# Padding in front of the MLP's inner activations: their SBUF addresses get the weight tiles' remainder modulo 512 bytes

## The chip, the cores and the metric

One core of one Trainium2 chip runs the whole program in one launch. The metric is the device time of one execution in microseconds (us), as the median over several runs. Engines are named as in the profile: PE is TensorE (PEld its weight loads), DVE is VectorE, ACT is ScalarE, POOL is GpSimd, SP issues most DMAs. SBUF addresses below are byte offsets within a partition, and "remainder" always means such an address modulo 512.

## The reference, cut to what matters

A decoder trunk of two layers works on 256 positions of width 2048, in float32. Each layer is a token mixer, a cross-attention to a memory of 256 positions, and an MLP, each behind an RMS norm and added to its input:

```python
for i in range(DEPTH):                      # DEPTH = 2
    h = rms_norm(x, g_mix[i])
    x = x + (chunked_gmlp(h, ...) if i % 2 == 0 else s5_glu(h, ...))
    x = x + memory_attention(rms_norm(x, g_xattn[i]), rms_norm(mem, g_mem[i]), ...)
    x = x + squared_relu_mlp(rms_norm(x, g_ff[i]), f_w_up[i], f_w_down[i])

def squared_relu_mlp(h, w_up, w_down):      # w_up 2048 x 8192, w_down 8192 x 2048
    return jnp.square(jax.nn.relu(h @ w_up)) @ w_down
```

The change lies in the MLP of both layers.

## The kernel before, in words

**How a product is made.** Every float32 operand of a large product is split into a high part in the type fp32r and a low part that holds the rest. A product is then three fp32r products: high by high, high by low, low by high. Weights stream from HBM in blocks of 512 KB (128 partitions by 1024 numbers). `wload` puts a block into one of four `wraw` tiles; `split` (L101, L102) lets ACT write the high part `whi` and DVE the low part `wlo`, of which there are three buffers each. On PE a matmul has a stationary operand, 128 columns that are loaded as weights, and a moving operand that streams past it, here 512 or 256 columns. All matmuls below are issued one after the other with the next one's weight load in between.

**The three shapes of the loop over a block.**
- `gemm_tok` (L145 to L147) multiplies activations in the large `act` tile with a weight block: the activations are stationary (`ah`, `al`), the weights move. It serves the mixers and the attention.
- `gemm_feat` (L163, L165) has it the other way round: the weights are stationary, the activations of `act` move. L163 takes high and low activations in one matmul of 512 columns, L165 one of 256. It makes the MLP's hidden values, and the attention's q and k.
- `gemm_hid` (L558 to L560) is written like `gemm_tok`, with the MLP's hidden values as stationary operand. These lie in tiles `hh` (high) and `hl` (low), four of each, that `mlp` allocates in a pool of its own. `gemm_last` (L579 to L581) does the same work for the very last quarter of columns in layer 1, with split weights that lie in two tiles `last`.

The inner lines of `gemm_tok` and of `gemm_hid`, in this order, are

```python
nc.tensor.matmul(out[t], ah[:, kt, sl], hi[:, kk, :], start=st, stop=False)             # L145
nc.tensor.matmul(out[t], ah[:, kt, sl], lo[:, kk, :], start=False, stop=False)          # L146
nc.tensor.matmul(out[t], al[:, kt, sl], hi[:, kk, :], start=False, stop=en)             # L147

nc.tensor.matmul(acc[:, t, :], ah[:, kt % 4, sl], hi[:, kk, :], start=st, stop=False)   # L558
nc.tensor.matmul(acc[:, t, :], ah[:, kt % 4, sl], lo[:, kk, :], start=False, stop=False)# L559
nc.tensor.matmul(acc[:, t, :], al[:, kt % 4, sl], hi[:, kk, :], start=False, stop=en)   # L560
```

The second argument is the stationary operand, the third the moving one. One weight block feeds 12 such matmuls, four groups of three; a group of three is called a triple below.

**The MLP.** The hidden width of 8192 is done in four rounds `b`. A round makes 2048 hidden values with eight calls of `gemm_feat` (each ends in a small `r` tile, from which ACT and DVE make `hh` and `hl`), and then multiplies them with a quarter of `f_w_down` in four calls of `gemm_hid`, 128 triples. In layer 0 the setup of the state-space mixer runs beside the MLP as small pieces (`side` work: DVE arithmetic, small matmuls, DMAs from POOL). In the last round of layer 1, the last 32 triples are those of `gemm_last`.

**What sets addresses.** Tiles of a pool lie one behind the other in the order in which they are first allocated, each start rounded up to 32 bytes. In the pool of `mlp` the first tile is `r2`, 8 bytes per partition, then come four `hh`, four `hl` and two `r`. The sizes of these are multiples of 512 bytes, so that all of them have one remainder, which depends on where the pool starts and on the size of `r2`. Columns are sliced from `act`, `hh`, `hl`, `whi` and `wlo` at multiples of 512 bytes, so the remainder of every operand of L145 to L147, L163, L165 and L558 to L560 is that of its tile.

**What sets the order.** The order on each engine is that of the program text, with side work put in at fixed ticks (one tick per weight block).

Of the kernel before, what the change touches and what calls it, by code (L numbers as in the profile page):

```python
# [9 lines left out]
F32 = mybir.dt.float32  # L10
# [6 lines left out]
P = 128  # L17
# [21 lines left out]
class Trunk:  # L39
# [470 lines left out]
    def mlp(self, x, layer, cur, nxt):  # L510
        nc, a, tc = self.nc, self.a, self.tc
        wu, wd = a["f_w_up"][layer], a["f_w_down"][layer]
        hT = cur.act
        with tc.tile_pool(name="ml", bufs=4, reuse_waits="tile") as mp:
            r2 = mp.tile([P, 2], F32, name="r2", bufs=1)
            for b in range(DFF // D):
                hid = []
                for n in range(NCH):
                    h = mp.tile([P, 4, S], F32R, name="hh")
                    l = mp.tile([P, 4, S], F32R, name="hl")  # L520
                    for i in range(2):
                        r = mp.tile([P, 2, S], F32, name="r", bufs=2)
                        self.gemm_feat(hT, wu, 2 * (NCH * b + n) + i, r)
                        nc.vector.scalar_tensor_tensor(out=r, in0=r, scalar=0.0, in1=r, op0=ALU.max, op1=ALU.mult)  # L524
                        self.split(h[:, 2 * i:2 * i + 2], l[:, 2 * i:2 * i + 2], r)
                    hid.append((h, l))
                if b == 0:
                    rstd = cur.rstd()
                    nc.vector.tensor_tensor(out=r2, in0=rstd, in1=rstd, op=ALU.mult)
                if b == DFF // D - 1:  # L530
                    nxt.start()
                for n in range(NCH):
                    if nxt.closing and b == DFF // D - 1 and n == NCH - 1:
                        self.gemm_last(hid, wd, n, b * KT, lambda t, acc: (
                            nc.vector.scalar_tensor_tensor(  # L535
                                out=x[:, t, n * NB:], in0=acc, scalar=r2[:, t:t + 1],
                                in1=x[:, t, n * NB:], op0=ALU.mult, op1=ALU.add), nxt.finish(x, t)))
                        break
                    acc = self.gemm_hid(hid, wd, n, b * KT)
                    for t in range(2):  # L540
                        xc = x[:, t, n * NB:(n + 1) * NB]
                        nc.vector.scalar_tensor_tensor(out=xc, in0=acc[:, t, :], scalar=r2[:, t:t + 1], in1=xc,  # L542
                                                       op0=ALU.mult, op1=ALU.add)
                    if b == DFF // D - 1:
                        self.at(1, lambda n=n: nxt.chunk(x, n))
# [647 lines left out]
```

## Time and profile before

| | |
|---|---|
| median of 3 runs | 2884.1 us (2883.07 to 2889.95) |
| the profiled execution's own time | 2886.18 us |
| its span, first to last instruction | 2884.4 us |
| PE busy in the span | 2837.0 us (98%) |
| DVE, ACT busy | 1831.7 us (64%), 1332.5 us (46%) |
| DMA | 579.55 MB, mean 201 GB/s |

A span is one execution on the core. A matmul's recorded duration (about 395 ns) overlaps that of the next, so the pace of a stream is read from start to start and not from durations. The MLP of layer 0 runs from about 690 to 1444 us of the span, that of layer 1 from 2155 to 2871 us.

### The profile page before, as it was taken

To read this page: it belongs to the slowest core of one execution; us is meant where nothing else is said; L and a number is where in the kernel's file an instruction comes from. 1 tells how busy PE (TensorE), PEld (TensorE's weight loads), DVE (VectorE), ACT (ScalarE), POOL (GpSimd) and SP (SyncE) were. 2 spreads that over 40 slices of the span, in tenths; PEclk is the share of its full clock that TensorE was granted. 3 is DMA by queue.
4 is the path that set the end of the run, shared out by engine and by line. 5 is a ranking of instruction groups with operands and counts; after the bars stand their busy time and mean duration, and the time that the engine had idled before them with its cause. 6 is when DMAs were issued, how large, how long until landed. Compare 5 with 4: busy or idle time off the path is not lost.

```text
span 2884.4 us, 39580 instructions
## 1 busy us (share of the span) xinstructions
PE 2837.0 (98%) x15238; PEld 2365.6 (82%) x15238; DVE 1831.7 (64%) x2548; ACT 1332.5 (46%) x1714; POOL 205.4 (7%) x384
## 2 busy tenths in 40 slices
PE   8999999999999999999989999999999999999998
PEld 6778888888878888788867788888888888888886
DVE  5665655575778878787567566555556555465555
ACT  5445544444534444444455445444454344343443
POOL 1000000000022222222011000000000000000000
PEclk9999999999999999999999999999999999999999
DMA  8656655558677777777689766655566566666665
GB/s 276 216 187 192 195 176 175 176 175 232 193 215 212 224 218 222 214 219 207 214 243 281 224 201 210 184 175 183 173 185 190 188 186 188 187 192 185 188 188 148
DMA packets 180461, 579.55 MB, mean 201 GB/s; under 512 B 37440, under 2 KB 39664, under 8 KB 179504
## 3 DMA queue, kind: packets, MB, share of 16 engines
q1 hardware_dynamic: 140864, 509.67, 57.3%
q0 software_dynamic: 39264, 67.29, 8.6%
q8 instruction: 119, 1.95, 0.3%
q14 instruction: 70, 0.57, 0.1%
q10 hardware_dynamic: 144, 0.07, 0.0%
HBM read 553.88 MB, written 22.94 MB: 200 GB/s over the span
## 4 chain that ended last, share of the span: by engine, by line
PE 90%; DMA 4%; DVE 3%; issue 2%; ACT 1%; POOL 0%; SPq 0%; DVEq 0%; ACTq 0%; POOLq 0%
PE acc L163 24%; PE acc L165 12%; PE acc L560 8%; PE acc L559 8%; PE acc L558 8%; PE acc L146 8%; PE acc L147 8%; PE acc L145 8%; DVE wlo L102 1%; DMA wraw<-in_b_w_in 1%; PE ps L494 1%; PE ps L438 1%; PE ps L214 1%; DMA memc<-in_mem 1%; DMA wraw<-in_f_w_up 0%
## 5 line engine op out<-in xcount | busy, mean ns | idle before, releaser
L102 DVE TENSOR_TENSOR wlo<-wraw,whi 128x1024 fp32r<-128x1024 f32 x952 | 1164.4, 1224 | 859.6 <-ACT whi L101 857.2
L101 ACT CAST whi<-wraw 128x1024 fp32r<-128x1024 f32 x952 | 999.5, 1051 | 1314.1 <-PE acc L163 394.0
L163 PE MATMUL acc<-act,whi 128*128 128x512 f32 x3072 | 1080.4, 395 | 0.6 <-ACT whi L101 0.6
L165 PE MATMUL acc<-act,wlo 128*128 128x256 f32 x3072 | 866.1, 282 | 1.7 <-DVE wlo L102 1.6
L163 PEld LDWEIGHTS acc<-act,whi 128*128 128x128 f32 x3072 | 576.1, 188 | 130.6 <-issue 1.6
L165 PEld LDWEIGHTS acc<-act,wlo 128*128 128x128 f32 x3072 | 581.5, 189 | 6.6 <-DVE wlo L102 2.9
L145 PE MATMUL acc<-whi,act 128*128 128x512 f32 x1248 | 493.8, 396 | 13.2 <-ACT whi L101 11.8
L146 PE MATMUL acc<-wlo,act 128*128 128x512 f32 x1248 | 493.1, 395 | 10.5 <-DVE wlo L102 10.4
L147 PE MATMUL acc<-whi,act 128*128 128x512 f32 x1248 | 490.8, 393 | 0.3 <-DVE act L102 0.3
L560 PE MATMUL acc<-whi,hl 128*128 128x512 f32 x992 | 395.3, 399 | 0.0
L558 PE MATMUL acc<-whi,hh 128*128 128x512 f32 x992 | 394.8, 398 | 0.0
L559 PE MATMUL acc<-wlo,hh 128*128 128x512 f32 x992 | 393.9, 397 | 0.0
L145 PEld LDWEIGHTS acc<-whi,act 128*128 128x128 f32 x1248 | 236.6, 190 | 65.3 <-ACT whi L101 14.3
L146 PEld LDWEIGHTS acc<-wlo,act 128*128 128x128 f32 x1248 | 236.6, 190 | 63.9 <-DVE wlo L102 16.9
L147 PEld LDWEIGHTS acc<-whi,act 128*128 128x128 f32 x1248 | 236.6, 190 | 48.5 <-DVE act L102 0.7
L559 PEld LDWEIGHTS acc<-wlo,hh 128*128 128x128 f32 x992 | 186.5, 188 | 46.4 <-issue 1.0
L560 PEld LDWEIGHTS acc<-whi,hl 128*128 128x128 f32 x992 | 186.5, 188 | 46.1 <-issue 1.6
L558 PEld LDWEIGHTS acc<-whi,hh 128*128 128x128 f32 x992 | 186.5, 188 | 44.7 <-issue 0.4
L809 POOL DMA_DIRECT2D Kd<-kd x128 | 72.4, 580 | 186.4 <-issue 174.2
L542 DVE SCALAR_TENSOR_TENSOR x<-acc,r,x 128x512 f32<-128x512 f32 x62 | 43.7, 746 | 10.6 <-PE acc L560 10.5
L176 ACT ACTIVATE junk<-x 128x512 f32<-128x512 f32 x56 | 35.3, 630 | 26.2 <-DVE x L535 14.0
L101 ACT CAST hh<-r 128x512 fp32r<-128x512 f32 x64 | 39.4, 615 | 16.6 <-DVE r L524 16.3
(288 smaller groups left out, 1663.2 us busy)
## 6 DMA issues: line engine op xcount, KB each, us to landing
wraw<-in_f_w_up SPq DMA_DIRECT2D x256, 512.0 KB, 3.7
wraw<-in_f_w_down SPq DMA_DIRECT2D x256, 512.0 KB, 3.7
wraw<-in_a_w_in SPq DMA_DIRECT2D x64, 512.0 KB, 4.4
wraw<-in_x_w_q SPq DMA_DIRECT2D x64, 512.0 KB, 3.7
wraw<-in_x_w_k SPq DMA_DIRECT2D x64, 512.0 KB, 3.6
wraw<-in_x_w_v SPq DMA_DIRECT2D x64, 512.0 KB, 3.7
wraw<-in_x_w_o SPq DMA_DIRECT2D x64, 512.0 KB, 3.7
wraw<-in_b_w_out SPq DMA_DIRECT2D x64, 512.0 KB, 4.4
```

The source lines that it names most:

```text
L101: self.nc.scalar.copy(out=hi, in_=src)
L102: self.nc.vector.tensor_tensor(out=lo, in0=src, in1=hi.bitcast(F32), op=ALU.subtract)
L145: nc.tensor.matmul(out[t], ah[:, kt, sl], hi[:, kk, :], start=st, stop=False)
L146: nc.tensor.matmul(out[t], ah[:, kt, sl], lo[:, kk, :], start=False, stop=False)
L147: nc.tensor.matmul(out[t], al[:, kt, sl], hi[:, kk, :], start=False, stop=en)
L163: nc.tensor.matmul(acc[:, f, :], hi[:, kk, sl], both[:, kt].rearrange("p a s -> p (a s)"), start=st, stop=False, skip_group_check=True)
L165: nc.tensor.matmul(acc[:, f, 0:S], lo[:, kk, sl], ah[:, kt, :], start=False, stop=en, skip_group_check=True)
L542: nc.vector.scalar_tensor_tensor(out=xc, in0=acc[:, t, :], scalar=r2[:, t:t + 1], in1=xc, op0=ALU.mult, op1=ALU.add)
L558: nc.tensor.matmul(acc[:, t, :], ah[:, kt % 4, sl], hi[:, kk, :], start=st, stop=False)
L559: nc.tensor.matmul(acc[:, t, :], ah[:, kt % 4, sl], lo[:, kk, :], start=False, stop=False)
L560: nc.tensor.matmul(acc[:, t, :], al[:, kt % 4, sl], hi[:, kk, :], start=False, stop=en)
L809: nc.gpsimd.dma_start(out=self.Kd[q // 2][:, :, q % 2, t], in_=kd[32 * t:32 * t + 16])
```

## The change

The first tile of the MLP's pool becomes wider and is used only in its first two columns: 56 numbers (224 bytes) in layer 0, 32 numbers (128 bytes) in layer 1, in place of 2 numbers (8 bytes).

```diff
         with tc.tile_pool(name="ml", bufs=4, reuse_waits="tile") as mp:
-            r2 = mp.tile([P, 2], F32, name="r2", bufs=1)
+            r2 = mp.tile([P, 32 if layer else 56], F32, name="r2", bufs=1)[:, 0:2]
             for b in range(DFF // D):
```

In the built programs this moves the tiles behind `r2`, and nothing else. The instructions of every engine, their order and their waits are the same in both programs. The addresses (first tile of each name) and remainders:

| tiles | before | remainder | after | remainder |
|---|---|---|---|---|
| `act`, both buffers | 37312, 70080 | 448 | the same | 448 |
| `whi`, `wlo`, `wraw`, all buffers | 119232, 131520, 102848 | 448 | the same | 448 |
| `last`, both (in the place of `act`) | 37312, 70080 | 448 | the same | 448 |
| layer 0: `hh`, `hl`, `r` | 187648, 204032, 220416 | 256 | 187840, 204224, 220608 | 448 |
| layer 1: `hh`, `hl`, `r` | 154464, 170848, 187232 | 352 | 154560, 170944, 187328 | 448 |

## Rows read from the trace of the kernel before

**Rows 1.** The profile's page: span, busy time, granted clock by slice, chain that ended last.

```profile
span 2884.4 us, 39580 instructions
PE 2837.0 (98%) x15238; PEld 2365.6 (82%) x15238; DVE 1831.7 (64%) x2548; ACT 1332.5 (46%) x1714; POOL 205.4 (7%) x384
...
PEclk9999999999999999999999999999999999999999
...
PE 90%; DMA 4%; DVE 3%; issue 2%; ACT 1%; POOL 0%; SPq 0%; DVEq 0%; ACTq 0%; POOLq 0%
```

**Rows 2.** Waits in layer 1's MLP, 2155 to 2871 us: total us, times, longest.

```profile
ACT whi L101 <- PE acc L560: 192.5, 113, 1.8
ACT whi L101 <- PE acc L163: 156.4, 98, 1.8
```

**Rows 3.** Stretches of the MLPs: length, PE, PEld, DVE, ACT, POOL busy; clock, DMA, GB/s.

```profile
780.70:875.20 94.50, 94.50 (x442) 74.68 (x441) 71.36 (x116) 39.76 (x48) 18.36 (x32) 1.00 0.70 210
...
2155.10:2243.80 88.70, 88.70 (x517) 78.40 (x516) 56.84 (x74) 42.83 (x54) 0.00 (x0) 1.00 0.61 190
2243.80:2333.40 89.60, 89.60 (x387) 72.11 (x386) 45.07 (x41) 34.54 (x34) 0.00 (x0) 1.00 0.60 188
2333.40:2423.80 90.40, 90.40 (x513) 78.49 (x512) 53.80 (x55) 40.62 (x46) 0.00 (x0) 1.00 0.61 187
2423.80:2513.40 89.60, 89.60 (x386) 72.14 (x385) 45.07 (x41) 34.56 (x34) 0.00 (x0) 1.00 0.62 188
2513.40:2602.20 88.80, 88.80 (x514) 78.38 (x513) 53.80 (x55) 40.65 (x46) 0.00 (x0) 1.00 0.61 190
...
2691.80:2782.10 90.30, 90.30 (x513) 78.40 (x512) 53.80 (x55) 40.62 (x46) 0.00 (x0) 1.00 0.63 187
```

**Rows 4.** Timeline of PE in `gemm_tok`, layer 1's attention: start us, duration us, instruction.

```profile
2113.09 0.39 PE L145 MATMUL acc<-whi,act 128*128 128x512 f32 x1
2113.32 0.39 PE L146 MATMUL acc<-wlo,act 128*128 128x512 f32 x1
2113.55 0.39 PE L147 MATMUL acc<-whi,act 128*128 128x512 f32 x1
2113.77 0.39 PE L145 MATMUL acc<-whi,act 128*128 128x512 f32 x1
...
2133.49 0.39 PE L145 MATMUL acc<-whi,act 128*128 128x512 f32 x1
```

**Rows 5.** Timeline of PE in `gemm_hid`, layer 1, first round.

```profile
2243.79 0.39 PE L558 MATMUL acc<-whi,hh 128*128 128x512 f32 x1
...
2331.99 0.39 PE L558 MATMUL acc<-whi,hh 128*128 128x512 f32 x1
2332.22 0.39 PE L559 MATMUL acc<-wlo,hh 128*128 128x512 f32 x1
2332.45 0.40 PE L560 MATMUL acc<-whi,hl 128*128 128x512 f32 x1
2332.69 0.39 PE L558 MATMUL acc<-whi,hh 128*128 128x512 f32 x1
```

**Rows 6.** Timeline of PE in `gemm_hid`, layer 0, last round, between two pieces of transposes.

```profile
1401.66 0.40 PE L558 MATMUL acc<-whi,hh 128*128 128x512 f32 x1
...
1422.66 0.39 PE L558 MATMUL acc<-whi,hh 128*128 128x512 f32 x1
```

**Rows 7.** `gemm_hid` by line, layer 1's first round: busy us, mean ns, idle before.

```profile
L560 PE MATMUL acc<-whi,hl 128*128 128x512 f32 x127 | 50.7, 399 | 0.0
L559 PE MATMUL acc<-wlo,hh 128*128 128x512 f32 x128 | 50.5, 394 | 0.0
L558 PE MATMUL acc<-whi,hh 128*128 128x512 f32 x128 | 50.2, 392 | 0.0
```

**Rows 8.** The same lines in the stretch of layer 0 that rows 6 show.

```profile
L558 PE MATMUL acc<-whi,hh 128*128 128x512 f32 x32 | 12.7, 397 | 0.0
L560 PE MATMUL acc<-whi,hl 128*128 128x512 f32 x32 | 12.6, 394 | 0.0
L559 PE MATMUL acc<-wlo,hh 128*128 128x512 f32 x32 | 12.6, 394 | 0.0
```

## The prediction

> **What bounds the kernel now.** I read the page first, then the waits inside the MLPs, then the MLPs cut into stretches, and last the starts of single matmuls. The page shows PE busy for 2837.0 of 2884.4 us, at the full clock of 2.4 GHz in every slice, and 90% of the chain that ended last is PE [rows 1]. A PE that is busy all the time can still be held up within its own stream, so the question is what sets the pace there. In layer 1's MLP no wait of PE appears; the waits are the other way round, the split of weights on ACT waiting for PE to release a buffer, 192.5 us in the `gemm_hid` stretches and 156.4 us in the `gemm_feat` stretches [rows 2]. So the weights are early and PE is late. The stretches say the same: PE is busy for all of each, DVE for 45.07 of 89.60 us, ACT for 34.54, the DMA engines for 0.60 of it [rows 3]. In layer 0 the side work brings DVE to 71.36 of 94.50 us, but PE is busy for all 94.50 there too.
>
> Now the pace. `gemm_tok` and `gemm_hid` issue the same triples of matmuls of the same shape on weights in the same buffers. In `gemm_tok` the starts of L145 run from 2113.09 to 2133.49 us over 30 triples, that is 20.40 / 30 = 0.680 us a triple [rows 4]. In `gemm_hid` of layer 1 the starts of L558 run from 2243.79 to 2332.69 us over 127 triples, 88.90 / 127 = 0.700 us [rows 5]; in layer 0, from 1401.66 to 1422.66 us over 30 triples, 21.00 / 30 = 0.700 us [rows 6]. So `gemm_hid` loses 20 ns on each triple, 6.7 ns on each matmul, with no idle time before any of them [rows 7, 8]. What differs between the streams is where the stationary operand lies: `act` has the remainder of `whi` and `wlo` (448), `hh` and `hl` have 256 in layer 0 and 352 in layer 1.
>
> That addresses matter on PE at all, I take from the durations by line. The same three lines of code last 392, 394 and 399 ns in layer 1, with the long one at L560 [rows 7], and 397, 394 and 394 ns in layer 0, spread otherwise [rows 8]. The code, the weight buffers and the clock are the same, the remainder is not.
>
> **The change part by part.** It adds no instruction and moves none; it moves `hh`, `hl` and `r` by 192 bytes in layer 0 and by 96 in layer 1. There are four things to price.
>
> First, the triples of `gemm_hid` and `gemm_last` with all remainders at 448. If they go at the pace of `gemm_tok`, each gains 0.700 - 0.680 = 0.020 us. Layer 1 has four rounds of 128, 512 triples in all: 512 x 0.020 = 10.2 us. The 32 of `gemm_last` are among them: their weights lie in `last`, remainder 448 as well, their stationary tiles are the same `hh` and `hl`. Layer 0 has as many, but the small matmuls of the side work cut in (442 PE instructions in the first stretch for 384 of `gemm_hid` [rows 3]), and a triple that is interrupted may gain less; I take 9.5 of the possible 10.2 us. Sum 19.7 us. All of it is on the path, since PE waits for nothing here. The bounds: nothing, if the remainder isn't what sets the pace, and 20.5 us (1024 x 0.020) if every triple gains.
>
> Second, what may be late next. A weight block now serves 4 x 0.680 = 2.72 us of PE, before 2.80 us. DVE is the fuller of the two engines that feed it, 45.07 of 89.60 us in layer 1; with the stretch at 128 x 0.680 = 87.0 us that is 52%. The DMAs would have to bring 188 x 89.6 / 87.0 = 194 GB/s, and they bring 210 in layer 0's stretch already [rows 3]. I put this cost at zero; the cover is that ACT waits for PE, in these same stretches, for 192.5 us. Without that cover PE would get back at most what the faster triples gave.
>
> Third, `gemm_feat` in the MLP. Its operands keep their addresses, yet it has two paces: eight calls take 88.70 and 88.80 us in rounds 0 and 2 of layer 1, and 90.40 and 90.30 us in rounds 1 and 3, with the same instructions and the full clock [rows 3]. The slower rounds stand behind a `gemm_hid` stretch that itself followed a faster one: something like a phase is carried from stream to stream, and a `gemm_hid` stretch flips it. The stretches of `gemm_hid` are 89.60 us long in either phase. If aligned streams no longer flip it, all four rounds go at the pace in which the MLP is entered. In this trace that is the faster one, and rounds 1 and 3 gain (90.40 - 88.70) + (90.30 - 88.80) = 3.2 us. If the MLP is entered in the slower phase, rounds 0 and 2 lose the same 3.2 us. In layer 0 up to three rounds behind a `gemm_hid` stretch could gain 1.6 us each, 4.8 us, but side matmuls cut into those too and I don't know their phase. Bounds for this term: 8.0 us gained to 3.2 us lost; I take the 3.2 us gained, the value nearest to the rows of layer 1, and nothing for layer 0.
>
> Fourth, DVE and ACT also read and write the moved tiles. Their operands `r`, `hh` and `hl` have one remainder among themselves before and after, so I see nothing that would change, and these engines are idle half of the time: zero, and a few us of work either way would be covered.
>
> The sum for the profiled execution: 2886.2 - 19.7 - 3.2 = 2863.3 us. That execution was 2.1 us above the median of the runs (2884.1), so the median should come to 2861.2; I round to 2862 because the third term is the less certain one.
>
> **A rule that speaks against it.** By rows 4 and 5 a stream of equal matmuls runs at 0.680 or at 0.700 us a triple, with no wait in either. The Trainium skill, in "TensorE: Matmul & The Clock Gate", section "Step-by-step: what each phase is for", says that PE has two independent SBUF read ports, one for the moving operand and one for weight loads, and that loading the next weights takes no read bandwidth from the running matmul. By that rule where the two operands lie relative to each other can't matter, and the time would stay at 2884. The rule leaves the 20 ns between the two streams without a reason, which is why I give it little.
>
> **The rivals.**
> *No change.* The two streams differ in other ways too: `ah` and `al` are interleaved in one tile in `gemm_tok` and 16 KB apart in `gemm_hid`, and the tiles lie in another region. If one of these makes the 20 ns, the padding changes nothing: 2884 us. For it speaks that no aligned `gemm_hid` exists in this trace; against it, that the spread over the lines differs between layers 0 and 1 whose tiles are spaced alike [rows 7, 8]. The rule of the Trainium skill above ends at this time too.
> *Half of it.* The pace depends on the address in a finer way, and only one layer, or only one or two of the three matmuls, gains. One layer alone gives 10 us: 2874; only the longest of three, some 7 ns a triple (399 against 392 [rows 7]), gives 1024 x 0.007 = 7 us: 2877. Against it: both layers get the very remainder that `act` has.
> *Slower.* Reads at one remainder get in each other's way when the tiles are separate ones. The place is L558 to L560. Every matmul would then take the longest step that these streams show, 0.24 us from L560 to the next L558 [rows 5], so 0.72 us a triple: 1024 x 0.020 = 20 us more, 2905. It decides from the point at which a triple takes over 0.700 us. Against it stands `gemm_tok`, where all operands have one remainder and the pace is the best of all.
>
> **How the numbers follow.** I give the forecast 0.82, no change 0.07, half of it 0.08, slower 0.03. Around the forecast the first term's bound (20.5) and the third's (8.0 gained, 3.2 lost) give 2884.1 - 28.5 = 2855.6 to 2884.1 - 9.5 - 10.2 + 3.2 = 2867.6. I stretch the upper end to 2872, to take in triples that gain only two thirds (19.7 x 2/3 = 13.1, 2871), and leave out the three other cases, 0.18 together. 0.3% is 8.7 us, about what a measurement of this kernel can tell from no change. Of the "half" case five eighths lie beyond it, so faster is 0.82 + 0.05 = 0.87; same is 0.07 + 0.03 = 0.10; slower 0.03.
>
> **What would show it.** In the profile after, starts of L558 0.680 us apart in both layers, stretches of `gemm_hid` in layer 1 of 87.0 us, mean durations of L558 to L560 near each other in both layers, and `gemm_feat` stretches of layer 1 all of one length, 88.8 us or 90.4 us (the third term). DVE and ACT busy times stay. It is wrong if the triples stay at 0.700 us in a layer, or if PE begins to wait for `whi` or `wlo` in the MLPs.

## The result, and the profile after

| | before | after |
|---|---|---|
| median, lowest and highest of 4 runs | 2883.59 us (2881.39 to 2889.95) | 2870.66 us (2866.36 to 2870.95) |
| the profiled execution | 2886.18 us | 2870.95 us |
| its span | 2884.4 us | 2869.2 us |

The ratio after to before is 0.9944, with a 95% interval of 0.9931 to 0.9956: 0.56% faster, clear of the 0.3% that can be told from no change. The forecast was 2862, with a range of 2855 to 2872. The kernel got faster for the reason given, but by 13 us, not 22.

The page of the kernel after, its span and busy times; as many instructions as before [rows 1], PE busy for 16.6 us less:

```profile
span 2869.2 us, 39580 instructions
...
PE 2820.4 (98%) x15238; PEld 2363.0 (82%) x15238; DVE 1831.1 (64%) x2548; ACT 1333.6 (46%) x1714; POOL 205.4 (7%) x384
```

The timeline of PE in `gemm_hid` of layer 1, first round, the first and the last start of L558 (127 triples apart), which answers to [rows 5]:

```profile
2237.02 0.39 PE L558 MATMUL acc<-whi,hh 128*128 128x512 f32 x1
...
2323.42 0.39 PE L558 MATMUL acc<-whi,hh 128*128 128x512 f32 x1
```

That is 86.40 / 127 = 0.680 us a triple, where it was 0.700. In layer 0, 30 triples apart, in the stretch of [rows 6]:

```profile
1397.06 0.39 PE L558 MATMUL acc<-whi,hh 128*128 128x512 f32 x1
...
1417.46 0.39 PE L558 MATMUL acc<-whi,hh 128*128 128x512 f32 x1
```

20.40 / 30 = 0.680 us as well, exactly `gemm_tok`'s pace in [rows 4]. The lines by mean duration in layer 1 (busy us, mean ns, idle before), against 399, 394 and 392 ns in [rows 7], have lost their spread:

```profile
L560 PE MATMUL acc<-whi,hl 128*128 128x512 f32 x128 | 49.8, 389 | 0.0
L559 PE MATMUL acc<-wlo,hh 128*128 128x512 f32 x128 | 49.8, 389 | 0.0
L558 PE MATMUL acc<-whi,hh 128*128 128x512 f32 x128 | 49.8, 389 | 0.0
```

The stretches, with the columns of [rows 3]; the first is a `gemm_hid` stretch of layer 0, then `gemm_feat` and `gemm_hid` of layer 1 take turns:

```profile
783.60:876.00 92.40, 92.40 (x442) 74.40 (x441) 71.21 (x116) 39.83 (x48) 18.37 (x32) 1.00 0.71 214
2148.30:2237.00 88.70, 88.70 (x516) 78.29 (x515) 56.84 (x74) 42.84 (x54) 0.00 (x0) 1.00 0.64 190
2237.00:2324.10 87.10, 87.10 (x386) 72.09 (x385) 45.05 (x41) 34.76 (x34) 0.00 (x0) 1.00 0.64 193
2324.10:2414.50 90.40, 90.40 (x513) 78.36 (x512) 53.79 (x55) 40.64 (x46) 0.00 (x0) 1.00 0.62 187
2414.50:2501.60 87.10, 87.10 (x386) 72.12 (x385) 45.05 (x41) 34.76 (x34) 0.00 (x0) 1.00 0.63 193
2501.60:2592.00 90.40, 90.40 (x513) 78.42 (x512) 53.79 (x55) 40.64 (x46) 0.00 (x0) 1.00 0.61 187
...
2679.10:2769.40 90.30, 90.30 (x512) 78.28 (x511) 53.79 (x55) 40.64 (x46) 0.00 (x0) 1.00 0.63 187
```

Two things are to be seen. Each `gemm_hid` stretch is 2.5 us shorter in layer 1 (87.10 for 89.60). And `gemm_feat`, whose operands have not moved, takes 90.4 us in round 2, where it took 88.80 in [rows 3]. It is slow in rounds 1, 2 and 3 now, and was slow in 1 and 3 before. With all stretches of both traces set side by side (a stretch from its first matmul to the next one's), the 15.2 us between the two spans come from here (the differences are those of the rounded lengths shown, good to 0.1 us):

| | before, us | after, us | difference |
|---|---|---|---|
| `gemm_hid`, layer 0, four rounds | 94.5, 94.2, 94.1, 93.2 | 92.4, 92.1, 92.1, 90.9 | -8.5 |
| `gemm_hid`, layer 1, four rounds (the last one to the end of the program) | 89.6, 89.6, 89.6, 102.2 | 87.1, 87.1, 87.1, 99.7 | -10.0 |
| `gemm_feat`, layer 0, four rounds | 93.4, 95.6, 95.8, 95.7 | 93.9, 95.4, 95.9, 95.6 | +0.3 |
| `gemm_feat`, layer 1, four rounds | 89.7, 90.4, 88.8, 90.4 | 89.7, 90.4, 90.4, 90.4 | +1.6 |
| everything else, with the way to the first matmul | | | +1.4 |

The largest part of the last line is the first `gemm_tok` stretch, before anything that moved, 297.8 us before and 299.2 after. It varies from execution to execution: 293.7 to 299.5 us in those executions below that leave its operands alone.

### The profile page after: what moved, and what is told of

Its sections match the earlier page's. It is cut to its first block, busy times and chain, and to the rows that moved or that the text cites. A ratio compares the mean times of both kernels' runs of the same rounds, so it can differ in the third digit from the quotient of the medians.

```text
span 2869.2 us, 39580 instructions
## 1 busy us (share of the span) xinstructions
PE 2820.4 (98%) x15238; PEld 2363.0 (82%) x15238; DVE 1831.1 (64%) x2548; ACT 1333.6 (46%) x1714; POOL 205.4 (7%) x384
## 4 chain that ended last, share of the span: by engine, by line
PE 91%; DMA 4%; DVE 2%; issue 2%; ACT 1%; POOL 0%; SPq 0%; DVEq 0%; ACTq 0%; POOLq 0%
PE acc L163 24%; PE acc L165 12%; PE acc L146 8%; PE acc L145 8%; PE acc L147 8%; PE acc L560 8%; PE acc L559 8%; PE acc L558 8%; DVE wlo L102 1%; PE ps L494 1%; DMA wraw<-in_b_w_in 1%; PE ps L438 1%; PE ps L214 1%; DMA memc<-in_mem 1%; PE ps L817 0%
## 5 line engine op out<-in xcount | busy, mean ns | idle before, releaser
L558 PE MATMUL acc<-whi,hh 128*128 128x512 f32 x992 | 388.8, 392 | 0.0
L560 PE MATMUL acc<-whi,hl 128*128 128x512 f32 x992 | 388.6, 392 | 0.0
L560 PEld LDWEIGHTS acc<-whi,hl 128*128 128x128 f32 x992 | 186.3, 188 | 40.3 <-issue 1.6
L558 PEld LDWEIGHTS acc<-whi,hh 128*128 128x128 f32 x992 | 186.2, 188 | 39.9 <-issue 0.4
```

## The experiments

Three questions were open. Is it the equal remainder, and is 512 its period? Does the gain come from both layers? And why did `gemm_feat` lose where 3.2 us were expected to be gained?

**Other distances for `hh` and `hl`.** Two kernels differ from the kernel after in the width of `r2` alone.

```diff
-            r2 = mp.tile([P, 32 if layer else 56], F32, name="r2", bufs=1)[:, 0:2]
+            r2 = mp.tile([P, 128 if layer else 120], F32, name="r2", bufs=1)[:, 0:2]
```

> hh and hl stand 256 bytes off the weight tiles' remainder in layer 0 (192 against 448) and 128 bytes off in layer 1 (320 against 448). Theory A, remainder: a triple of gemm_hid takes 0.680 us only where the stationary and the moving tile have the same remainder modulo 512; so 0.700 us in both layers, gemm_hid stretches of layer 1 of 89.6 us, and a time near the kernel before (2883). Rival B, a shorter period: if the same remainder modulo 256 is enough, layer 0 goes at 0.680 us, and if modulo 128 is enough, both do (2871).

One run: 2874.44 us. The timeline of this kernel's PE, L558 in layer 0 (30 triples apart), then in layer 1 (127 triples apart):

```profile
1393.92 0.39 PE L558 MATMUL acc<-whi,hh 128*128 128x512 f32 x1
...
1414.33 0.39 PE L558 MATMUL acc<-whi,hh 128*128 128x512 f32 x1
...
2233.53 0.39 PE L558 MATMUL acc<-whi,hh 128*128 128x512 f32 x1
...
2322.06 0.39 PE L558 MATMUL acc<-whi,hh 128*128 128x512 f32 x1
```

In layer 0, at a distance of 256 bytes, 20.41 / 30 = 0.680 us: as good as an equal remainder. In layer 1, at 128 bytes, 88.53 / 127 = 0.697 us: nearly all of the loss. Rival B was right with 256: an equal remainder modulo 256 is enough for the fast pace, it need not be equal modulo 512, and theory A had to give way to an A2 that says so.

The second kernel takes distances of 64 and 32 bytes:

```diff
-            r2 = mp.tile([P, 32 if layer else 56], F32, name="r2", bufs=1)[:, 0:2]
+            r2 = mp.tile([P, 24 if layer else 40], F32, name="r2", bufs=1)[:, 0:2]
```

> hh and hl stand 64 bytes off the weight tiles' remainder in layer 0 (384) and 32 bytes off in layer 1 (416). Theory A: 0.700 us a triple in both layers, as soon as the remainders differ at all. Rival B: modulo 64 is enough, then layer 0 goes at 0.680 us and layer 1 not. A third way: the loss grows with the distance, then layer 1 lies between 0.680 and 0.700 us, at 32/96 of the loss of the kernel before about 0.687.

One run: 2881.84 us. Its timeline, the same four places:

```profile
1395.71 0.39 PE L558 MATMUL acc<-whi,hh 128*128 128x512 f32 x1
...
1416.31 0.39 PE L558 MATMUL acc<-whi,hh 128*128 128x512 f32 x1
...
2237.80 0.39 PE L558 MATMUL acc<-whi,hh 128*128 128x512 f32 x1
...
2326.70 0.39 PE L558 MATMUL acc<-whi,hh 128*128 128x512 f32 x1
```

At 64 bytes (layer 0) 20.60 / 30 = 0.687 us, between the two; at 32 bytes (layer 1) 88.90 / 127 = 0.700 us, the whole loss. So an equal remainder modulo 128, 64 or 32 is not enough, and the loss doesn't grow with the distance: 32 bytes cost more than 64. That the pace at 64 lies between was foreseen by none of the three.

The same trace has something on `gemm_feat` too. Its stretches in rounds 1, 2 and 3 of layer 1 are all slow, as in the kernel after, though `gemm_hid` is not aligned here and runs at 0.700 us:

```profile
2327.40:2417.80 90.40, 90.40 (x513) 78.44 (x512) 53.79 (x55) 40.62 (x46) 0.00 (x0) 1.00 0.62 187
2507.40:2597.80 90.40, 90.40 (x513) 78.35 (x512) 53.79 (x55) 40.61 (x46) 0.00 (x0) 1.00 0.59 187
2687.50:2777.90 90.40, 90.40 (x513) 78.35 (x512) 53.79 (x55) 40.62 (x46) 0.00 (x0) 1.00 0.61 187
```

In the first kernel, at 128 bytes, the same three rounds are slow, fast and slow, as in [rows 3]:

```profile
2322.80:2413.20 90.40, 90.40 (x513) 78.44 (x512) 53.81 (x55) 40.65 (x46) 0.00 (x0) 1.00 0.60 187
2502.40:2591.10 88.70, 88.70 (x513) 78.16 (x512) 53.80 (x55) 40.67 (x46) 0.00 (x0) 1.00 0.61 190
2680.40:2770.80 90.40, 90.40 (x513) 78.34 (x512) 53.79 (x55) 40.64 (x46) 0.00 (x0) 1.00 0.61 187
```

**The weights moved instead.** The kernel after with 96 bytes in front of the weight tiles. `hh` and `hl`, which lie behind them, move along; `act` stays.

```diff
-        self.wp = ent(tc.tile_pool(name="wp", bufs=3))
+        self.wp = ent(tc.tile_pool(name="wp", bufs=3)); self.wp.tile([P, 24], F32, name="pad", bufs=1)
```

> The kernel after with 96 bytes put in front of the weight tiles: whi, wlo and, behind them, hh and hl all have remainder 32 now, act keeps 448. Theory A (only the difference counts): gemm_hid stays at 0.680 us a triple at the new common remainder, gemm_tok goes from 0.680 to 0.700 us, 1280 triples or 25.6 us more, and gemm_feat, whose operands differ now too, leaves its 0.347 us a pair by an amount that I can't derive, between nothing and 13 ns a pair (3072 pairs, 41 us): 2896 to 2937 in all. Rival C (the absolute place of the stationary tile counts, 448 is a good one): gemm_tok stays at 0.680 us since act has not moved, gemm_hid falls back to 0.700 us, 2884 or so.

2877.86 us median of 8, ratio to the kernel before 0.9974 (95% interval 0.9963 to 0.9985). The timeline of `gemm_tok` in layer 1's attention, 30 triples apart:

```profile
2095.54 0.40 PE L145 MATMUL acc<-whi,act 128*128 128x512 f32 x1
...
2116.55 0.39 PE L145 MATMUL acc<-whi,act 128*128 128x512 f32 x1
```

21.01 / 30 = 0.700 us, where [rows 4] have 0.680: `act` has not moved, the weights have. The stretches of this kernel in layer 1, `gemm_hid` of round 0 and then `gemm_feat` of rounds 1, 2 and 3:

```profile
2250.60:2337.70 87.10, 87.10 (x386) 72.13 (x385) 45.05 (x41) 34.76 (x34) 0.00 (x0) 1.00 0.62 193
2337.70:2426.50 88.80, 88.80 (x514) 78.17 (x513) 53.78 (x55) 40.69 (x46) 0.00 (x0) 1.00 0.61 190
2513.50:2602.30 88.80, 88.80 (x514) 78.13 (x513) 53.78 (x55) 40.69 (x46) 0.00 (x0) 1.00 0.61 190
2689.30:2778.00 88.70, 88.70 (x513) 78.07 (x512) 53.78 (x55) 40.69 (x46) 0.00 (x0) 1.00 0.61 190
```

`gemm_hid` keeps its 87.1 us at another absolute place (remainder 32), so it is the distance between stationary and moving tile that counts, not the place of one of them; rival C is out. The time itself missed the expectation, and that was the find: with the weights 96 bytes above `act` (modulo 512), `gemm_feat` did not lose but went at its faster pace in every round. Over the program, against the kernel before, the stretches of `gemm_tok` grew by 19.6 us (25.6 were expected) and those of `gemm_hid` and `gemm_feat` shrank by 18.0 and 7.7.

**Layer 1 alone.**

```diff
-            r2 = mp.tile([P, 32 if layer else 56], F32, name="r2", bufs=1)[:, 0:2]
+            r2 = mp.tile([P, 32 if layer else 2], F32, name="r2", bufs=1)[:, 0:2]
```

> The padding in layer 1 alone; layer 0 has hh and hl at remainder 256 as before. By the stretches of the traces before and after, layer 1 gains 4 x 2.5 us in gemm_hid and loses 1.6 us in the gemm_feat of round 2: 8.4 us less than before, 2876. Layer 0's gemm_hid stretches are 2.0 to 2.3 us longer each than in the kernel after, 8.5 us. If the gain of 12.9 us came from one layer alone, this run shows all of it (2871) or nothing (2884).

2875.48 us median of 6, ratio 0.9972 (0.9960 to 0.9983). The stretches of `gemm_hid` in layer 0 (round 0) and layer 1 (round 0), and of `gemm_feat` in layer 1's round 2:

```profile
776.60:871.10 94.50, 94.50 (x443) 74.40 (x442) 71.41 (x116) 39.72 (x48) 18.36 (x32) 1.00 0.71 210
...
2241.70:2328.80 87.10, 87.10 (x387) 72.11 (x386) 45.04 (x41) 34.76 (x34) 0.00 (x0) 1.00 0.63 192
...
2506.30:2596.70 90.40, 90.40 (x513) 78.43 (x512) 53.78 (x55) 40.65 (x46) 0.00 (x0) 1.00 0.59 187
```

As expected: layer 0 is back at 94.5 us, layer 1 keeps 87.1, and round 2 of `gemm_feat` is slow with layer 1's padding alone. Both layers give their part: by the medians layer 1 alone is worth 8.7 us and layer 0 another 5.6, by the stretches 8.4 and 8.5.

**A break in front of `gemm_feat`.** The kernel after with one small matmul between the streams of layer 1.

```diff
                     if b == DFF // D - 1:
                         self.at(1, lambda n=n: nxt.chunk(x, n))
+                if layer and b < 3: nc.tensor.transpose(self.ps([P, 2, S])[:, 0, :P], self.ident, self.ident)
```

> The kernel after with one matmul more in layer 1 behind each of the first three gemm_hid stretches, a transpose of 128 columns of the identity into a tile that nobody reads. It costs some 0.1 to 0.3 us a time. Theory A2 (the pace of gemm_feat is carried over from the stream before it): a break can set it anew, so at least one of rounds 1 to 3 leaves 90.4 us for 88.8 us. Rival (the pace belongs to the round itself): all three stay at 90.4 us. If all three stay, a break that sets the same pace again isn't excluded.

One run: 2866.71 us. The stretches of `gemm_feat` in rounds 1, 2 and 3:

```profile
2321.20:2411.70 90.50, 90.50 (x514) 78.46 (x513) 53.78 (x55) 40.63 (x46) 0.00 (x0) 1.00 0.61 187
2498.80:2587.70 88.90, 88.90 (x515) 77.80 (x514) 53.79 (x55) 40.65 (x46) 0.00 (x0) 1.00 0.62 190
2674.80:2765.30 90.50, 90.50 (x515) 78.55 (x514) 53.79 (x55) 40.63 (x46) 0.00 (x0) 1.00 0.60 186
```

The break itself costs about 0.1 us. Round 2 went to the faster pace, 1 and 3 did not. So one matmul in between can set the pace of the 512 that follow, and the pace doesn't belong to the round; but a break doesn't set it to the fast one by itself. Slow, fast, slow is the order that the kernel before shows without a break [rows 3]. That this run is 4.2 us shorter than the profiled one of the kernel after is not the break's doing: its first stretch alone is 5.5 us shorter (293.7 us).

**The same program twice, and a version that beats both.** The kernel after was run again beside a kernel that keeps its `gemm_hid` and takes over what the moved weights had shown. The buffers of `act` become 256 bytes longer, and only the MLPs' `act` begins 160 bytes into its buffer. Seen modulo 256, the weights then stand 96 above it in `gemm_feat` of the MLPs, 0 in `gemm_tok` and in `gemm_hid`.

```diff
-    def new_act(self):
-
-        a = self.act.tile([P, KT, 2, S], F32R, name="act")
+    def new_act(self, off=0):
+        a = self.act.tile([P, 64 + KT * 2 * S], F32R, name="act")[:, off:off + KT * 2 * S]
+        a = a.rearrange("p (k a s) -> p k a s", k=KT, a=2)
...
-        self.act = self.tr.new_act()
+        self.act = self.tr.new_act(40 if self.gi >= 6 else 0)
```

> The kernel after once more, on the same chip as the others of this call: 2871 us, 0.994 of the kernel before. gemm_feat of layer 1 in rounds 1 to 3 at 90.4 us if its pace is settled by what the program does, at 88.8 us in some of them if it is settled by chance.

> The kernel after, with the act tile of the two MLPs moved inside a buffer that is 256 bytes longer, so that the weight tiles stand 96 bytes (modulo 256) above it for gemm_feat; gemm_tok sees a difference of 0 or 256, gemm_hid of 0. Theory A2 (equal remainder modulo 256 is the fast case for gemm_tok and gemm_hid; for gemm_feat a difference of 96 has one pace, 0.347 us a pair, while a difference of 0 has two, 0.347 and 0.353, and keeps the one in which it is entered): gemm_feat of layer 1 takes 88.8 us in all four rounds, 4.8 us less than in the kernel after (rounds 1 to 3), layer 0 gains 1.5 + 0.2 + 1.2 + 0.8 = 3.7 us as in the run with the weights moved; gemm_tok stays at 0.680 us: 8 us below the kernel after, 2862. Rival: the slow pace of gemm_feat is made by something else in the rounds (buffers, DVE and ACT at work), the run with the weights moved was fast for its later start; then rounds 1 to 3 stay at 90.4 us and the time at 2871.

The kernel after again: 2869.86 us median of 5, ratio 0.9949 (0.9937 to 0.9962). Its `gemm_feat` of layer 1 in rounds 1 to 3:

```profile
2323.80:2414.20 90.40, 90.40 (x514) 78.35 (x513) 53.78 (x55) 40.64 (x46) 0.00 (x0) 1.00 0.60 187
...
2501.30:2591.70 90.40, 90.40 (x514) 78.44 (x512) 53.78 (x55) 40.64 (x46) 0.00 (x0) 1.00 0.60 187
2678.80:2769.20 90.40, 90.40 (x513) 78.36 (x512) 53.78 (x55) 40.64 (x46) 0.00 (x0) 1.00 0.62 187
```

Slow in the same three rounds, so it wasn't chance. The new version: 2858.44 us median of 4, ratio 0.9914 (0.9900 to 0.9927). Its stretches of `gemm_hid` (round 0) and `gemm_feat` (rounds 1, 2 and 3) in layer 1:

```profile
2228.50:2315.60 87.10, 87.10 (x387) 72.08 (x386) 45.03 (x41) 34.76 (x34) 0.00 (x0) 1.00 0.61 193
2315.60:2404.40 88.80, 88.80 (x514) 78.16 (x513) 53.78 (x55) 40.70 (x46) 0.00 (x0) 1.00 0.61 190
2491.40:2580.20 88.80, 88.80 (x514) 78.19 (x513) 53.78 (x55) 40.70 (x46) 0.00 (x0) 1.00 0.62 190
2667.20:2756.00 88.80, 88.80 (x514) 78.19 (x513) 53.78 (x55) 40.70 (x46) 0.00 (x0) 1.00 0.63 190
```

All rounds are at the faster pace, 4.8 us less than in the kernel after; `gemm_hid` has what the padding gave it; `gemm_feat` of layer 0 is 3.7 us shorter than in the run beside it (92.2, 94.7, 94.7 and 94.8 us against 92.9, 95.7, 95.9 and 95.6). That is 8.5 of the 11.4 us between the two medians; most of what else differs between the two traces (3.5 us) lies in the first stretch of the program, which the edit isn't meant to touch.

## Why the prediction was right, and where it was not

*What bounds.* Right. PE set the end before and after, and what its stream loses inside shows in no wait. The gain lies in the `gemm_hid` stretches to 0.02 us a triple.

*First term, the triples.* Right, and a little too large: 19.7 us foreseen, 18.5 measured (8.5 in layer 0 for 9.5, 10.0 in layer 1 for 10.2). The reason given, an equal remainder, is shown by the runs with other distances and with the weights moved; that it must be equal modulo 512 is not so, modulo 256 is enough. One premise on the way to it does not hold, though. The prediction took from the spread of durations over the lines that addresses matter on PE: L560 the longest in layer 1 [rows 7], L558 in layer 0 [rows 8], with only the remainder different. But in the very next round of layer 1 in the same trace, at the same remainder, it is L558 that is longest (2423.9 to 2513 us):

```profile
L558 PE MATMUL acc<-whi,hh 128*128 128x512 f32 x128 | 51.1, 399 | 0.0
L559 PE MATMUL acc<-wlo,hh 128*128 128x512 f32 x128 | 50.2, 392 | 0.0
L560 PE MATMUL acc<-whi,hl 128*128 128x512 f32 x127 | 50.1, 394 | 0.0
```

So the spread changes from round to round, as the pace of `gemm_feat` does, and could not tell the remainder from anything else, nor speak against "no change". What was left were the paces of [rows 4] to [rows 6], which fit the other differences between the two streams as well. That it was the remainder was to that extent luck; the runs that moved addresses decided it.

*Second term, what is late next.* Right. In layer 1's MLP no wait of PE appears after either, and ACT still waits for PE there, if less than the 192.5 and 156.4 us of [rows 2] together:

```profile
ACT whi L101 <- PE acc L560: 182.9, 113, 1.7
ACT whi L101 <- PE acc L163: 157.7, 98, 1.8
```

*Third term, `gemm_feat`.* Wrong in sign, though inside the bounds that it was given: 3.2 us of gain foreseen, 1.6 us of loss measured in layer 1, and 0.3 in layer 0, which is less than a layer 0 round differs between executions (round 0 took 92.0 to 95.2 us in the runs above with the same operands). The step that failed is "If aligned streams no longer flip it, all four rounds go at the pace in which the MLP is entered". That the pace is carried from stream to stream was right: the break moved it in one round, and round 2 changed in the kernel after with no operand of its own moved. What did not hold was the premise that alignment ends the flip: in the kernel after, an aligned `gemm_hid` stream turns the faster pace into the slower one, and does not turn it back. Nor is it alignment that decides: at 32 bytes off, not aligned, the rounds went the same way, and at 128 bytes off they alternated. In layer 1, behind a fast round 0, round 1 was slow in all seven traces in which `gemm_feat` had its operands at a distance of 0; round 2 was slow in four of them and fast in three. The step was argued from the alternation in [rows 3] alone, and no aligned `gemm_hid` stood in that trace. The sign that the prediction named, all four rounds of layer 1 of one length, did not come either: round 0 stayed fast.

In layer 1 this term makes up 4.8 of the 7.6 us by which the profiled execution (2870.95) missed the 2863.3 of the sum; the triples are 1.2, layer 0's `gemm_feat` 0.3, and the remaining 1.3 lie in stretches that the change doesn't touch.

*Fourth term.* Right: DVE was busy for 1831.1 us after 1831.7, ACT for 1333.6 after 1332.5.

*The offset to the median.* The profiled execution of before stood 2.6 us over its final median, that of after 0.3 us. So the 2.1 us that were taken off were 1.8 too many; rounding up to 2862 gave 0.8 of them back. That is the 1.0 us that is left of the 8.7 us between forecast and median.

*The rivals.* "No change", and with it the rule of the Trainium skill that the two SBUF read ports of PE are independent and loading the next weights takes no read bandwidth from the running matmul ("TensorE: Matmul & The Clock Gate", "Step-by-step: what each phase is for"), does not describe these streams: with nothing but addresses moved, a triple goes from 0.700 to 0.680 us, and back to 0.697 or 0.700 at other distances, while the tiles stay 16 KB apart and in their own region. "Half of it" and "slower" had their mechanisms refuted by 0.680 us in both layers.

## What to carry to other kernels

Compare the pace of equal matmuls between loops, from start to start: a difference of 20 ns in 700, with no wait before any of them, was worth 0.6% of a kernel whose PE was busy for 98% of the time. Where a stationary and a moving tile come from different pools, look at the remainders of their addresses, and pick them for each pairing, since here `gemm_hid` wanted 0 and `gemm_feat` went better at 96, the only distance other than 0 that was tried for it. When a stream has two paces with the same operands, don't count on the better one: find the placement that has only one.

## What the runs showed of the hardware that was not expected

- For triples of 512-column fp32r matmuls, with the stationary tile's remainder modulo 512 minus the moving tile's: 0 and 256 give 0.680 us; 448 gives 0.687; 384 gives 0.697; 320, 416 and 480 give 0.700. The loss has no order by distance. Other distances were not tried, and why the pace depends on the distance at all stays open.
- `gemm_feat`, alternating 512 and 256 columns, has two paces at a distance of 0, 88.8 / 256 = 0.347 and 90.4 / 256 = 0.353 us a pair, and in layer 1 holds one for a whole stretch. At 96 only the faster one was seen, in all MLP rounds of layer 1 in two kernels. What is carried from stream to stream stays open, and so does why `gemm_hid` streams at a distance of 0 or 480 lead into the slower pace in rounds 1 to 3, while behind those at 384 and 416, and at 0 with a break, it alternates.
